# Storing the adaLN gates of a two-layer hybrid trunk: one transposed store a layer instead of column stores

## The chip, the core and the metric

The kernel runs on one core of a Trainium2 chip. The metric is device time in microseconds (us) of one execution; lower is better. The core has a matrix engine, TensorE (PE), and three engines for elementwise work, VectorE (DVE), ScalarE (ACT) and GpSimd (POOL). Each works through its own queue in order. Transfers are issued from SyncE (SP), from ACT and from POOL, and are moved by 16 DMA engines that all of these share. On-chip tiles have 128 partitions; what PE writes goes to PSUM, everything else is in SBUF or in device memory (DRAM).

## The reference

Two trunk layers run over 512 latent tokens and 256 context tokens, each of width 1024. Each layer begins by modulating its input with vectors that depend on the conditioning, and ends by gating its output with another of these vectors:

```
mod   = silu(c)     @ mod_w[l] + mod_b[l]        # 3 x 1024: shift, scale, gate (latents)
mod_c = silu(c_ctx) @ mod_w[l] + mod_b[l]        # the same for the context tokens
z   = (rmsnorm(x, pre_g) * (1 + scale) + shift) @ w_in
y_mla, y_pool, y_gla = attention(z), pooling mixer(z), gated linear attention(z)
out = (g_m * (y_mla @ w_bm) + g_p * (y_pool @ w_bp) + g_g * (y_gla @ w_bg)) @ w_out
x   = x + gate * rmsnorm(out, post_g)
```

The context stream does the same with mod_c, in layer 0 only; layer 1 uses the context for keys, values and states but does not produce it. The result is the latent stream after layer 1.

## The kernel before

All large products are made in three terms from operands that are split into a high and a low part (`mm3`): ACT makes the high part (`wh`, `act`), DVE the low part (`wl`, `tt`). Weights come in loads of 512 KB, issued on SP (`load_raw`, line 106), into a ring of three buffers with the tag "raw" in the pool `stream`; the split frees the buffer.

In each layer the projection is computed in blocks (`z_A`, `z_B`; the merge gates are the blocks `zA_m`, weights `raw_m`), staged through the pool `stage` (tag "st", two buffers) and written to DRAM by POOL's queue. The merge gates are interleaved with the attention heads (queries, scores `sc`, softmax `pe`, transposes `pt`, weighted sums `av`). Then the three branches are projected and merged (`br_p`, `br_g`, `br_m`; their inputs `yp`, `yg`, `ym` are reloaded through the same "raw" ring), and last come the output projection (`zB_wo`, `wo`), the post norm, the gate and the residual.

The function `modulation(l)` computes the 3072 modulation values of layer l in twelve chunks of 256 columns. Chunks 0 to 3 are the shift, 4 to 7 the scale, 8 to 11 the gate. It is a generator, and the layers advance it at fixed places. Layer 0's first eight chunks are made on PE at the start of the program. All others are made beside PE (`chunk_beside_pe`): the weight chunk comes in two halves through the "raw" ring (`raw_mod`), DVE and POOL accumulate 128 partial sums (`macc`), and four or eight small products with a column of ones (`modt`, in a PSUM tile of the pool `psz`, tag "z", two buffers) sum over the partitions. So the result stands as columns: partition p, column b holds value 128 b + p. The function `columns` adds the bias and, for the gate chunks, multiplies with the post norm's gain; the result lies in `cols` (in the profile `mcols`), for two streams (latents and context; in layer 1's gate chunks only the latents).

Shift and scale are used as columns. The gate is needed as a row that is the same on all partitions, since it multiplies tiles whose partitions are tokens. For that, each gate chunk is written to a DRAM tensor `grow` of shape 2 x 1024, one store per stream, each from 128 partitions with two values of 4 bytes (line 180):

```
nc.gpsimd.dma_start(out=grow[st].rearrange("(b p) -> p b", p=P)[:, 2 * j - 16:2 * j - 14], in_=dst[:, :, st])
```

and before the output projection `gate_rows` (line 265) reads each row back, the same 4 KB to all 128 partitions, into the tile `pg`. `pg` is used in the multiplications of `part` and `xo` by the gate (lines 1056 and 1072).

Layer 0's four gate chunks, the eight chunks of layer 1's shift and scale, and the first of its gate chunks are made in layer 0, beside its attention and at the start of its merge; the other three gate chunks of layer 1 are made in layer 1, beside the projection of the pooling branch.

The order of the instructions on every engine is not the order of the text: a planner reorders the whole program when it is built, from simulated times of the instructions and from priorities that the text sets (`urgent`).

Of the kernel before, what the change touches and what calls it, by code (L numbers as in the profile page):

```python
# [11 lines left out]
F32 = mybir.dt.float32  # L12
# [6 lines left out]
P = 128  # L19
D = 1024  # L20
KD = 8
# [4 lines left out]
DEPTH = 2  # L26
# [22 lines left out]
def hybrid_kernel(ctx, tc, io, out):  # L49
    nc = tc.nc  # L50
    V, S, G, PE = nc.vector, nc.scalar, nc.gpsimd, nc.tensor
# [8 lines left out]
    stage = ctx.enter_context(tc.tile_pool(name="stage", bufs=2))  # L60
    small = ctx.enter_context(tc.tile_pool(name="small", bufs=4))
    dram = ctx.enter_context(tc.tile_pool(name="dram", bufs=1, space=MemoryType.DRAM))
    psz = ctx.enter_context(tc.tile_pool(name="psz", bufs=2, space=MemoryType.PSUM))
# [3 lines left out]
    def act(out, in_, func=AF.Copy, **kw):  # L67
        return S.activation(out=out, in_=in_, func=func, **kw)  # L68

    def tt(out, a, b, op=ALU.mult, eng=None):  # L70
        return (eng or V).tensor_tensor(out=out, in0=a, in1=b, op=op)  # L71

    def stt(out, a, s, b, op0=ALU.mult, op1=ALU.mult):
        return V.scalar_tensor_tensor(out=out, in0=a, scalar=s, in1=b, op0=op0, op1=op1)  # L74
# [13 lines left out]
    def mm(out, lhsT, rhs, start, stop):  # L88
        PE.matmul(out=out, lhsT=lhsT, rhs=rhs, start=start, stop=stop)  # L89
# [14 lines left out]
    def load_raw(src, nk, width, name, pool=stream):  # L104
        raw = pool.tile([P, nk, width], F32, tag="raw", name=f"raw_{name}", bufs=3 if pool is stream else None)
        nc.sync.dma_start(out=raw, in_=src)
        return raw
# [17 lines left out]
    ident = const.tile([P, P], F32, name="ident")  # L125
# [29 lines left out]
    def modulation(l, pool=None):  # L155


        cols = const.tile([P, 24, 2], F32, tag=f"mcols{l}", name=f"mcols{l}")
        grow = dram.tile([2, D], F32, name=f"grow{l}")
        mods[l] = (cols, grow)  # L160
        modb = small.tile([P, 24], F32, tag="modb", name=f"modb{l}", bufs=1)
        nc.gpsimd.dma_start(out=modb, in_=io["mod_b"][l])
        pre = small.tile([P, KD], F32, tag="pre", name=f"pre{l}", bufs=1)
        nc.gpsimd.dma_start(out=pre, in_=io["pre_norm"][l])
        post = small.tile([P, KD], F32, tag="post", name=f"post{l}", bufs=1)
        nc.gpsimd.dma_start(out=post, in_=io["post_norm"][l])

        def columns(j, pt, streams=2):

            at = slice(2 * j, 2 * j + 2)  # L170
            dst = cols[:, at, 0:streams]

            def spread(v, c0):
                return v[:, 2 * j - c0:2 * j - c0 + 2].unsqueeze(2).to_broadcast([P, 2, streams])

            tt(dst, pt[:, :, 0:streams], spread(modb, 0), ALU.add)
            if j >= 8:
                tt(dst, dst, spread(post, 16))
                for st in range(streams):
                    nc.gpsimd.dma_start(out=grow[st].rearrange("(b p) -> p b", p=P)[:, 2 * j - 16:2 * j - 14], in_=dst[:, :, st])  # L180
            elif j >= 4:

                stt(dst, dst, 1.0, spread(pre, 8), ALU.add, ALU.mult)

        def chunk_on_pe(j):
            parts = j in (5, 6, 3, 7)
            ps = pst.tile([4 if parts else 2, 256], F32, tag="t", name=f"modps{l}_{j}")
            for half in range(2):
                raw = pool.tile([P, 4, 256], F32, tag="raw", name=f"raw_mod{l}_{j}_{half}", bufs=10)
                nc.sync.dma_start(out=raw, in_=io["mod_w"][l, j][:, 4 * half:4 * half + 4, :])  # L190
                if parts:
                    wh = pool.tile([P, 4, 256], F32R, tag="xin", name=f"mwh{l}_{j}_{half}", bufs=6)
                    wl = pool.tile([P, 4, 256], F32R, tag="xin", name=f"mwl{l}_{j}_{half}", bufs=6)
                    act(wh, raw)
                    tt(wl, raw, wh.bitcast(F32), ALU.subtract)
                for k in range(4):
                    kk = 4 * half + k
                    if parts:
                        mm(ps, chl[:, kk, :], wh[:, k, :], kk == 0, False)
                        mm(ps[0:2], chl[:, kk, 0:2], wl[:, k, :], False, kk == KD - 1)  # L200
                    else:
                        mm(ps, csil[:, kk, :], raw[:, k, :], kk == 0, kk == KD - 1)
            n = 4 if parts else 2
            row = pool.tile([n, 256], F32, tag="modrow", name=f"modrow{l}_{j}")
            act(row, ps)
            pt = psz.tile([P, 2, 2], F32, tag="z", name=f"modt{l}_{j}")
            for i in range(2):
                mm(pt[:, i], row[:, i * P:(i + 1) * P], sel[0:n], True, True)
            columns(j, pt)

        def chunk_beside_pe(j):

            streams = 2 if j < 8 or l < DEPTH - 1 else 1
            acc = small.tile([P, 2, 256], F32, tag="macc", name=f"macc{l}_{j}", bufs=1)
            for half in range(2):
                raw = load_raw(io["mod_w"][l, j][:, 4 * half:4 * half + 4, :], 4, 256, f"mod{l}_{j}_{half}")
                for k in range(4):
                    kk = 4 * half + k
                    for st in range(streams):
                        c = csil[:, kk, st:st + 1]  # L220
                        w, a = raw[:, k], acc[:, st]
                        eng = (G if streams == 1 and kk%2 else V) if st==0 else (G if kk%2 else V)
                        if kk == 0:
                            (eng if eng is G else V).tensor_scalar(out=a, in0=w, scalar1=c, scalar2=None, op0=ALU.mult)
                        elif eng is V:
                            stt(a, w, c, a, ALU.mult, ALU.add)
                        else:
                            if eng is S:
                                act(w, w, scale=c)
                            else:  # L230
                                G.tensor_scalar(out=w, in0=w, scalar1=c, scalar2=None, op0=ALU.mult)  # L231
                            tt(a, a, w, ALU.add, G)
            yield
            pt = psz.tile([P, 2, 2], F32, tag="z", name=f"modt{l}_{j}")
            for i in range(2):
                for st in range(streams):
                    mm(pt[:, i, st:st + 1], acc[:, st, i * P:(i + 1) * P], ones, True, True)
            columns(j, pt, streams)


        pend = []
        for j in (0, 4, 1, 5, 2, 6, 3, 7, 8, 9, 10, 11):
            if pool is not None and j < 8:
                chunk_on_pe(j)
            else:
                pend.append(chunk_beside_pe(j))
                next(pend[-1])
                if len(pend) > 1:
                    next(pend.pop(0), None)
            if j == 11 or (pool is None and j == 7):  # L250
                yield
                for chunk in pend:
                    next(chunk, None)
                pend = []
            yield

    mods = {}

    def gate_rows(l, pool, streams):

        grow = mods[l][1]
        res = []
        for s in range(streams):
            pgt = pool.tile([P, D], F32, tag=f"pg{s}", name=f"pg{l}_{s}", bufs=1)
            nc.gpsimd.dma_start(out=pgt, in_=grow[s].partition_broadcast(P))
            res.append(pgt)
        return res

# [81 lines left out]
    def layer(l, hT, close_hT, side, todo_mod):  # L350
# [680 lines left out]
        op = g6.enter_context(opened(f"outp{l}", 2, side))  # L1031
        psw = g6.enter_context(opened(f"psw{l}", 4, None, MemoryType.PSUM))
        pgr = gate_rows(l, op, 2 if full else 1)
        part = op.tile([P, NT, 512], F32, tag="part", name=f"part{l}", bufs=1)
        order = [2, 3, 4, 5] + ([0, 1] if full else [])
# [74 lines left out]
    sp = g0.enter_context(opened("start", 2, "left"))  # L1110
    psx = g0.enter_context(opened("psx", 4, None, MemoryType.PSUM))
    mod0 = modulation(0, sp)
    xin = {}
    for t in (2, 3, 4, 5, 0, 1):
# [28 lines left out]

    close_hT, side = gh.close, "left"
    todo_mod = chain(mod0, *(modulation(l) for l in range(1, DEPTH)))
    for l in range(DEPTH):
        hT, close_hT = layer(l, hT, close_hT, side, todo_mod)
# [108 lines left out]
```

## Time and profile before

| | |
|---|---|
| median of 3 runs | 1515.74 us (1512.39 to 1519.95) |
| the profiled execution | 1514.81 us, span 1513.0 us |
| granted TensorE clock, mean | 0.984 |
| busy: PE, PEld, DVE, ACT, POOL | 95%, 85%, 71%, 47%, 34% |
| moved by DMA | 209.75 MB, mean 139 GB/s |
| stores to grow (line 180) | 12, 1.0 KB each, issue to landing 9.4 us in the median |
| reads of grow (line 265) | 3, 512 KB each, 4.7 us in the median |

The profile is of one execution. PEld is PE's loading of the stationary operand, which overlaps with its products. An instruction's row names its line, its operation and the tiles it writes and reads (`out<-in`); where a helper issues it, the line is the helper's (line 68 is `act`, 71 `tt`, 74 `stt`, 89 `mm`). In square brackets stands how long the engine was idle before the instruction and which engine, line and tile ended that wait. In tables by window the busy time of each engine is followed by the number of its instructions, and after the engines come the granted clock of TensorE (1.00 is full speed), the busy share of the 16 DMA engines and the GB/s that they moved. For transfers the time from issue to landing is given.

### The profile page before, as it was taken

The page shows a single profiled execution, that of the slowest core. Times are in us where ns is not written, and L with a number is a line of the kernel's source. Part 1 is how long each engine was busy: PE and PEld are TensorE (multiplying, and loading weights), DVE is VectorE, ACT ScalarE, POOL GpSimd, SP SyncE. Part 2 cuts the span into 40 slices and gives each one's busy share as a digit, 9 for nine tenths or more (in the row PEclk, how much of TensorE's full clock was granted, in tenths as well). Part 3 has the DMA queues.
Part 4 walks back from the last instruction along what each step waited for, and adds up shares of the span by engine and source line. Part 5 has one row for each costly group of instructions (what it writes and reads, how often), then busy time and mean ns, then how long its engine had stood idle before and what let it go on. Part 6 is the DMA issues. An engine that isn't in the chain of part 4 may idle for free.

```text
span 1513.0 us, 23911 instructions
## 1 busy us (share of the span) xinstructions
PE 1444.7 (95%) x8940; PEld 1279.7 (85%) x8940; DVE 1066.7 (71%) x1980; ACT 717.3 (47%) x1340; POOL 521.8 (34%) x695
## 2 busy tenths in 40 slices
PE   7999999999997999997999999999999999998988
PEld 4799899998886889886879988988988888886778
DVE  3645999757576788876676373789976676686783
ACT  6554453343334445666443345654253555454532
POOL 3432333444243443542111064414463100053550
PEclk9999999999998999998999999999999999999999
DMA  9333323256544532346565234334356523157731
GB/s 366 108 125 113 107 96 115 90 166 192 183 74 101 144 118 90 130 147 163 173 210 198 82 126 129 124 127 127 100 180 204 164 96 96 51 151 145 232 132 69
DMA packets 64195, 209.75 MB, mean 139 GB/s; under 512 B 12464, under 2 KB 15696, under 8 KB 64080
## 3 DMA queue, kind: packets, MB, share of 16 engines
q1 hardware_dynamic: 38688, 116.74, 25.2%
q0 software_dynamic: 24528, 88.34, 18.3%
q10 hardware_dynamic: 864, 3.15, 0.5%
q8 instruction: 70, 1.15, 0.3%
q14 instruction: 45, 0.37, 0.1%
HBM read 161.65 MB, written 46.54 MB: 138 GB/s over the span
## 4 chain that ended last, share of the span: by engine, by line
PE 63%; issue 11%; DVE 11%; DMA 8%; POOL 3%; ACT 3%; POOLq 0%; DVEq 0%; SPq 0%; ACTq 0%
PE zA_m L89 13%; PE zB_gv L89 5%; PE zA_px L89 4%; PE zA_mg L89 4%; PE zB_wo L89 4%; PE wo L89 3%; DMA raw_m<-in_w_in 3%; PE lv L89 3%; PE zA_pg L89 3%; PE zA_gk L89 2%; PE br_p L89 2%; PE br_m L89 2%; PE br_g L89 2%; PE zB_qkv L89 2%; PE zA_gq L89 2%
## 5 line engine op out<-in xcount | busy, mean ns | idle before, releaser
L89 PE MATMUL zA_m<-hh,wh_m 128*128 128x512 f32 (+1 forms) x576 | 206.6, 359 | 1.0 <-ACT wh_m L68 1.0
L89 PE MATMUL zA_m<-hh,wl_m 128*128 128x512 f32 (+1 forms) x576 | 206.7, 359 | 0.6 <-DVE wl_m L71 0.6
L89 PE MATMUL zA_m<-hl,wh_m 128*128 128x512 f32 (+1 forms) x576 | 206.5, 359 | 0.0
L89 PEld LDWEIGHTS zA_m<-hh,wh_m 128*128 128x128 f32 x576 | 110.1, 191 | 16.0 <-ACT wh_m L68 1.4
L89 PEld LDWEIGHTS zA_m<-hh,wl_m 128*128 128x128 f32 x576 | 109.9, 191 | 15.6 <-DVE wl_m L71 1.1
L89 PEld LDWEIGHTS zA_m<-hl,wh_m 128*128 128x128 f32 x576 | 109.9, 191 | 14.4
L68 ACT ACTIVATE wh_m<-raw_m 128x1024 fp32r<-128x1024 f32 x48 | 50.9, 1060 | 93.0 <-PE zA_m L89 45.5
L68 ACT ACTIVATE pe<-sc,mx 128x768 f32<-128x768 f32 (+1 forms) x80 | 65.2, 814 | 60.2 <-DVE mx L831 59.7
L831 DVE TENSOR_REDUCE mx<-sc 128x1 f32<-128x768 f32 (+1 forms) x80 | 67.7, 846 | 34.7 <-PE sc L89 34.0
L71 DVE TENSOR_TENSOR wl_m<-raw_m,wh_m 128x1024 fp32r<-128x1024 f32 x48 | 59.0, 1228 | 45.6 <-ACT wh_m L68 45.1
L231 POOL TENSOR_SCALAR raw_mod<-raw_mod,csil 128x256 f32<-128x256 f32 x64 | 69.2, 1085 | 62.0 <-DVE macc L74 38.5
L74 DVE SCALAR_TENSOR_TENSOR macc<-raw_mod,csil,macc 128x256 f32<-128x256 f32 x132 | 70.8, 547 | 12.4 <-POOL macc L71 10.5
L68 ACT ACTIVATE pth<-pt 128x256 fp32r<-128x256 f32 (+1 forms) x144 | 61.8, 471 | 34.6 <-PE pt L853 34.0
L71 DVE TENSOR_TENSOR ptl<-pt,pth 128x256 fp32r<-128x256 f32 (+1 forms) x144 | 72.6, 534 | 7.2 <-ACT pth L68 6.2
L89 PEld LDWEIGHTS lv<-pqk 128*128 128x128 f32 x560 | 70.8, 191 | 4.7 <-issue 1.8
L347 POOL DMA_DIRECT2D sm<-st_m x32 | 17.6, 550 | 165.5 <-ACT st_m L68 148.1
L89 PE MATMUL lv<-pqk 128*128 128x128 f32 x560 | 73.4, 275 | 1.3 <-DVE pqk L71 1.2
L89 PE MATMUL sc<-kth,qth 96*128 96x256 f32 (+1 forms) x144 | 50.8, 353 | 19.0 <-ACT pe L68 18.9
L71 POOL TENSOR_TENSOR macc<-macc,raw_mod 128x256 f32<-128x256 f32 x64 | 55.1, 860 | 36.4 <-DVE macc L74 30.6
L89 PE MATMUL br_p<-yp,wh_wbp 128*128 128x512 f32 (+1 forms) x192 | 56.3, 376 | 8.6 <-ACT yp L68 6.8
L853 PE MATMUL pt<-ident,pe 128*128 128x128 f32 x416 | 61.3, 273 | 0.7 <-ACT pe L68 0.7
L89 PE MATMUL zB_gv<-wh_gv,hh 128*128 128x256 f32 x192 | 55.7, 291 | 4.1 <-ACT st_gv L68 2.1
(402 smaller groups left out, 4732.8 us busy)
## 6 DMA issues: line engine op xcount, KB each, us to landing
raw_mod<-in_mod_w SPq DMA_DIRECT2D x48, 512.0 KB, 5.0
raw_m<-in_w_in SPq DMA_DIRECT2D x48, 512.0 KB, 3.8
sm<-st_m POOLq DMA_DIRECT2D x24, 384.0 KB, 2.9
raw_wo<-in_w_out SPq DMA_DIRECT2D x16, 512.0 KB, 4.0
sm<-st_m POOLq DMA_DIRECT2D x24, 256.0 KB, 2.5
raw_gv<-in_w_gv SPq DMA_DIRECT2D x8, 512.0 KB, 4.6
raw_gg<-in_w_in SPq DMA_DIRECT2D x8, 512.0 KB, 4.0
raw_px<-in_w_in SPq DMA_DIRECT2D x8, 512.0 KB, 3.7
```

The lines of the kernel that those rows point to most:

```text
L68: return S.activation(out=out, in_=in_, func=func, **kw)
L71: return (eng or V).tensor_tensor(out=out, in0=a, in1=b, op=op)
L74: return V.scalar_tensor_tensor(out=out, in0=a, scalar=s, in1=b, op0=op0, op1=op1)
L89: PE.matmul(out=out, lhsT=lhsT, rhs=rhs, start=start, stop=stop)
L231: G.tensor_scalar(out=w, in0=w, scalar1=c, scalar2=None, op0=ALU.mult)
L347: nc.gpsimd.dma_start(out=dst[:, lo:T], in_=st[:, lo:T])
L831: V.tensor_reduce(out=mx, in_=ps[:, 0:nkey], axis=AX.X, op=ALU.max, negate=True)
L853: PE.transpose(out=pt[:, kk, :], in_=pe[:, (k0 + kk) * P:(k0 + kk + 1) * P], identity=ident)
```

## The change

The twelve column stores go. `grow` gets the shape 8 x streams x 128, with two streams in layer 0 and one in layer 1. After the last gate chunk of a layer, PE transposes the gate columns (128 x 16 in layer 0, 128 x 8 in layer 1) into a PSUM tile of `psz`, ACT copies the 16 or 8 rows of 128 values into a tile of `stage`, and one store on POOL's queue writes them to `grow`. The reads in `gate_rows` follow the new layout: a row of 1024 values lies in DRAM as eight pieces of 128 values, in layer 0 every second such piece, in layer 1 one behind the other.

```diff
@@ modulation
-        grow = dram.tile([2, D], F32, name=f"grow{l}")
+        grow = dram.tile([KD, 2 if l < DEPTH - 1 else 1, P], F32, name=f"grow{l}")
@@ columns
             if j >= 8:
                 tt(dst, dst, spread(post, 16))
-                for st in range(streams):
-                    nc.gpsimd.dma_start(out=grow[st].rearrange("(b p) -> p b", p=P)[:, 2 * j - 16:2 * j - 14], in_=dst[:, :, st])
@@ modulation, the loop over chunks
                 for chunk in pend:
                     next(chunk, None)
                 pend = []
+            if j == 11:
+
+                n = KD * grow.shape[1]
+                pt = psz.tile([n, P], F32, tag="z", name=f"gateT{l}")
+                columns_ = cols[:, 16:24, :].rearrange("p b s -> p (b s)") if n > KD else cols[:, 16:24, 0]
+                PE.transpose(out=pt, in_=columns_, identity=ident)
+                row = stage.tile([P, P], F32, tag="st", name=f"gates{l}")
+                act(row[0:n], pt)
+                nc.gpsimd.dma_start(out=grow.rearrange("b s p -> (b s) p"), in_=row[0:n])
             yield
@@ gate_rows
-            nc.gpsimd.dma_start(out=pgt, in_=grow[s].partition_broadcast(P))
+            nc.gpsimd.dma_start(out=pgt.rearrange("q (b p) -> q b p", p=P), in_=grow[:, s].partition_broadcast(P))
```

## The prediction

> **What bounds the kernel now.** I read the page's busy times first, then the idle stretches of TensorE in the tables by window, then for each long stretch the releaser in the timelines, and last the transfers under way at that moment.
>
> ```profile
> PE 1444.7 (95%) x8940; PEld 1279.7 (85%) x8940; DVE 1066.7 (71%) x1980; ACT 717.3 (47%) x1340; POOL 521.8 (34%) x695
> ```
>
> TensorE (PE) is busy 95% of the span, so it sets the time, and a saving has to come from its idle time or its clock. The three longest holes that have a gate store just ahead of them look like this (columns: window, its length, busy time of PE, PEld, DVE, ACT, POOL, then granted clock, busy share of the DMA engines, GB/s):
>
> ```profile
> 444.00:452.60 8.60, 8.60 (x53) 7.56 (x51) 7.92 (x13) 1.55 (x5) 3.72 (x5) 1.00 1.00 35
> 452.60:462.90 10.30, 0.08 (x2) 0.04 (x1) 1.07 (x1) 2.13 (x4) 0.00 (x0) 0.67 0.52 85
> 462.90:466.50 3.60, 3.60 (x16) 3.60 (x17) 3.15 (x8) 1.15 (x3) 1.47 (x1) 0.51 0.42 146
> ...
> 699.40:706.30 6.90, 0.07 (x2) 0.02 (x1) 1.00 (x2) 0.70 (x2) 1.74 (x3) 0.69 0.65 122
> 706.30:712.20 5.90, 5.89 (x17) 4.68 (x18) 4.59 (x11) 5.33 (x12) 0.28 (x1) 0.50 0.76 253
> ...
> 1373.30:1378.10 4.80, 0.05 (x2) 0.03 (x1) 0.93 (x1) 2.01 (x4) 0.00 (x0) 0.97 0.59 206
> 1378.10:1384.70 6.60, 6.20 (x18) 5.14 (x19) 6.38 (x11) 4.96 (x9) 3.75 (x4) 0.51 0.57 167
> ```
>
> PE stands still for 10.2, 6.8 and 4.8 us, and each time it restarts at half clock. Ahead of the first hole the 16 DMA engines are busy all the time (share 1.00) and yet move 35 GB/s. What ended each hole, and what POOL had issued before:
>
> ```profile
> 443.70 1.48 POOL L180 DMA_DIRECT2D grow<-mcols  x2
> 460.74 1.06 ACT L68 ACTIVATE wh_m<-raw_m 128x1024 fp32r<-128x1024 f32 x1 [13.88 <-DMA raw_m<-in_w_in]
> 461.82 0.90 ACT L68 ACTIVATE pe<-sc,mx 128x768 f32<-128x768 f32 x1
> 462.87 0.58 PE L89 MATMUL sc<-kth,qth 96*128 96x256 f32 x1 [10.22 <-ACT pe L68]
> ...
> 692.75 0.74 POOL L180 DMA_DIRECT2D grow<-mcols  x1 [0.32 <-DVE mcols L71]
> 705.60 1.88 ACT L68 ACTIVATE yp<-yrp 128x512 fp32r<-128x512 f32 x4 [7.40 <-DMA yrp<-yp]
> 706.28 1.81 PE L89 MATMUL br_p<-yp,wh_wbp 128*128 128x512 f32 x3 [6.83 <-ACT yp L68]
> ...
> 1363.63 0.75 POOL L180 DMA_DIRECT2D grow<-mcols  x1
> 1376.09 1.06 ACT L68 ACTIVATE wh_wbp<-raw_wbp 128x1024 fp32r<-128x1024 f32 x1 [10.04 <-DMA raw_wbp<-in_w_branch_p]
> 1378.08 0.80 PE L89 MATMUL sc<-kth,qth 96*128 96x512 f32 x1 [4.75 <-ACT pe L68]
> ```
>
> The pattern is the same three times: POOL issues a store to grow, ScalarE (ACT) then waits 7 to 14 us for a load that should be quick, and PE waits behind ACT, because ACT works its queue in order (the softmax pe of the first and third hole sits behind the split of the weights). Issue to landing, first over the whole run, then in the windows around the three stores (440 to 462, 690 to 699, 1360 to 1370):
>
> ```profile
> L180 POOL DMA_DIRECT2D grow<-mcols x12: 716/742/776, 426.4 to 1387.1; - x12
> DMA to landing us min/median/max: 7.1/9.4/16.6
> ...
> raw_m<-in_w_in SPq DMA_DIRECT2D x48, 512.0 KB, 3.8
> raw_wbp<-in_w_branch_p SPq DMA_DIRECT2D x8, 512.0 KB, 4.5
> sm<-st_m POOLq DMA_DIRECT2D x24, 384.0 KB, 2.9
> DMA to landing us min/median/max: 2.5/3.0/10.9
> ...
> raw_m<-in_w_in SPq DMA_DIRECT2D x1, 512.0 KB, 16.2
> sm<-st_m POOLq DMA_DIRECT2D x1, 384.0 KB, 12.6
> raw_wbp<-in_w_branch_p SPq DMA_DIRECT2D x1, 512.0 KB, 11.2
> ```
>
> The first two rows are those of the stores at L180: 1 KB each, 9.4 us in the median. The second "DMA to landing" row is that of yrp. While such a store is under way, loads that take 3 to 4.5 us take 11 to 16. So the stores of 256 packets of 4 bytes hold the DMA engines, everything queued beside them waits, and PE runs dry where it has too little in hand. That it can have enough is seen beside two others, with PE busy throughout:
>
> ```profile
> 483.39 1.51 POOL L180 DMA_DIRECT2D grow<-mcols  x2
> 483.00:493.00 10.00, 10.00 (x60) 8.68 (x59) 9.62 (x22) 5.67 (x14) 8.21 (x10) 1.00 0.51 60
> ...
> 1346.90 0.76 POOL L180 DMA_DIRECT2D grow<-mcols  x1 [0.31 <-DVE mcols L71]
> 1346.90:1356.40 9.50, 9.50 (x57) 8.29 (x56) 9.36 (x19) 3.68 (x9) 6.47 (x8) 1.00 0.49 69
> ```
>
> So the price of a store is what PE lacks at that moment, not its 9 us; I count only the three holes.
>
> **The change part by part.**
>
> *Removed: twelve stores (eight in layer 0, four in layer 1).* POOL is relieved of 12 x 0.74 us = 8.9 us of issuing (the median in the row of L180). POOL is 34% busy and ends none of the three holes, so I count that at nothing; it only brings the macc sums behind the stores forward by 0.7 to 1.5 us.
>
> The holes, one by one, with what is late next:
>
> ```profile
> 444.53 0.33 SPq L106 DMA_DIRECT2D raw_m<-in_w_in  x1
> ...
> 689.96 16.98 SPq L935 DMA_DIRECT2D yrp<-yp  x4
> ...
> 1356.28 8.87 SPq L106 DMA_DIRECT2D raw_wbp<-in_w_branch_p  x2
> ```
>
> Hole 1. raw_m, issued at 444.53, lands after 3.8 us at 448.3; the split (1.06) and the softmax behind it (0.90, both rows above) are done by 450.3, before PE needs them at 452.65. DVE's half of the split is next; DVE is busy 7.92 of the 8.6 us up to 452.6, so it comes perhaps 0.5 us late. Recovered: 10.22 of waiting, and 3.6 us at clock 0.51 that cost 3.6 x 0.49 = 1.8: 12.0 - 0.5 = 11.5 us.
>
> Hole 2. The second of four yrp loads is the late one; at 3.0 us it lands at about 698.2 and PE asks for it at 699.45. But the loads share a ring of three buffers (tag "raw") with the last weights of the modulation, so they come one at a time, load 3.0 plus ACT's split of 0.94 (half of the 1.88 above) apiece, and the four cannot all be there at 700. I leave 3.5 us of the hole standing: 6.83 + 5.9 x 0.50 - 3.5 = 6.3 us.
>
> Hole 3. The second raw_wbp is issued at 1356.28 + 8.87 - 0.33 = 1364.8 and lands after 4.5 at 1369.3; split and softmax take 2 us, to 1371.3, before PE needs them at 1373.3. Recovered: 4.75 + 6.6 x 0.49 = 8.0 us.
>
> Together 11.5 + 6.3 + 8.0 = 25.8 us. Of it the half clock is 1.8 + 2.95 + 3.2 = 7.95. The Trainium skill, page "TensorE: Matmul & The Clock Gate", Part 1, says that about 3.4 us of work after an idle window run at half clock; that is an estimate of 1.7 us a restart, 5.1 in all, and a sum 2.9 us smaller. Of the three restarts here one agrees (3.6 us), two last 5.9 and 6.6, so I stay with the rows.
>
> *Added: one transpose, one copy and one store of rows per layer.* PE's work is small:
>
> ```profile
> L853 PE MATMUL pt<-ident,pe 128*128 128x128 f32 x416 | 61.3, 273 | 0.7 <-ACT pe L68 0.7
> 1380.16 0.85 PE L89 MATMUL modt<-ones,macc 128*128 128x1 f32 x4
> ...
> 1386.60 0.16 DVE L71 TENSOR_TENSOR mcols<-mcols,post 128x2 f32<-128x2 f32 x1
> ```
>
> 2 x 0.27 = 0.5 us of PE. The wait matters more: the transpose needs the last product with post, and PE works in order, so whatever stands behind the transpose waits for DVE too. In layer 1 that product ended 1386.76 - 1381.01 = 5.75 us after modt. The wait lies between 0 (the planner puts it late enough) and 5.75 a layer; the planner reckons with DVE's queue as well, so I take the lower part, 1 us a layer. The transpose takes one of the two "z" buffers of PSUM that the zA blocks turn over, and the copy one of the two "st" buffers, behind which a later evacuation (st_m) may wait for a landing of 2.9: between 0 and 2.9 a layer, and I put it inside that 1 us, since stage_out does the same dozens of times beside a busy PE. The new stores are 16 and 8 rows of 512 bytes; their POOL issue is bounded by 0.74. Total 0.5 + 2 = 2.5 us.
>
> *Moved: the gates are stored once, after the last chunk.* The reader is far behind:
>
> ```profile
> 816.87 0.53 POOL L265 DMA_DIRECT2D pg<-grow  x1 [1.46 <-PE br_g L89]
> L71 DVE TENSOR_TENSOR part<-part,pg x10: 684/692/693, 845.0 to 1485.9; 128x512 f32<-128x512 f32 x10
> osg<-sgg POOLq DMA_DIRECT2D x10, 256.0 KB, 3.5
> ```
>
> Layer 0 has stored long before 692.75, where layer 1's first store stands, and reads at 816.87. In layer 0 the read now takes 1024 pieces of 512 bytes where it took 128 of 4 KB. The nearest row is osg, 512 pieces of 512 bytes in 3.5 us; twice that is at most 7 us, and the first use is at 845.0, 28 us after the issue. I cost it at nothing; without that cover it would be 2 x 7 = 14 us. Layer 1's rows lie side by side, so its read is as before.
>
> *Sum.* 25.8 - 2.5 = 23.3. The profiled execution took 1514.81 us (span 1513.0), 0.9 under the median 1515.74. 1514.8 - 23.3 = 1491.5; I put 1492. The bounds: all three holes with their clock (21.8 + 7.95 = 29.7) and no cost give 1485; the short holes beside them could add a few us, so 1482. Holes closed by half and both waits at the transposes at their upper end give 1514.8 - 14.9 + 12 = 1512; I take 1508 as the upper end for 8 in 10.
>
> One term has no row. The order on every engine comes from a planner that reckons the whole program with times of its own; with twelve stores fewer it may come out another way from about 425 us on. I give it no sign; its size is bounded by one hole like these, 8 to 12 us either way.
>
> **The rivals.**
>
> *Partial.* The loads become quick, but another wait takes over: the ring of three raw buffers, which POOL's slow sums release, or PE standing at the transposes. For it: hole 2, where four loads share the ring. Against it: in holes 1 and 3 the late load had already been issued 8 us or more before PE ran dry. It recovers 8 to 17 us: 1498 to 1507, say 1503.
>
> *No change.* The loads are late for a reason that stays (the ring, the planner's order), and the stores only fall in the same stretch. Then the cost of 2.5 remains: 1517. For it: beside the stores at 483 and 1347 PE has no hole. Against it: loads with a landing of 11 to 16 us stand beside stores each time, with the DMA engines full at 35 GB/s. The Trainium skill, page "DMA: Bandwidth & Descriptors", section "Anatomy of one DMA", gives about 2.0 us plus bytes over 436 GB/s for a transfer issued from GpSimd, so a store of 1 KB would take 2.0 us and hold up little; by that rule this rival would be the forecast. The trace has 9.4 us, and I go by it.
>
> *Slower.* The pieces of 512 bytes do to the loads what those of 4 bytes did. A store's 256 pieces are 16 for each of 16 engines in 9.4 - 2.9 = 6.5 us, 0.41 us a piece; 64 pieces each would be 26 us, twice 52, beginning at 817 beside the loads of w_out. The readers of pg are covered until 845, 28 us, the weights that are loaded beside it by little, so the stall is between 24 and 52; with the middle, 38, and 3 of clock, 1492 + 41 = 1533. It is slower by half a per cent from about 0.33 us a piece on. Against it: osg moves 512 such pieces in 3.5 us, some 0.1 us a piece at most.
>
> **How the numbers follow.** Forecast, 1483 to 1498: 0.60. Partial, 1498 to 1508: 0.22. No change: 0.11. Slower: 0.05. More than the three holes, under 1483: 0.02. Half a per cent, which is about what a measurement of this kernel can tell, is 7.6 us: faster means below 1508, slower above 1523. So faster 0.84, same 0.11, slower 0.05. The range 1482 to 1508 leaves out the last cases.
>
> **What would show it.** Right: no load of 512 KB in layer 0's attention above some 7 us; the holes near 452 and 1373 gone, with no half clock there; a shorter one near 700; the landing of grow near 3 us; pg under 8 us; two new transposes with less than 2 us of PE idle ahead of them. Wrong: holes of the same size with normal landings (then the order is to blame), landings still long with no grow store beside them, or PE idle for several us at the transposes with DVE's mcols as the releaser.

## The result, and the profile after

| | before | after |
|---|---|---|
| median | 1515.74 us (1512.39 to 1519.95) | 1492.08 us (1491.12 to 1495.41) |
| profiled execution, span | 1514.81, 1513.0 us | 1491.12, 1489.3 us |
| granted clock, mean | 0.984 | 0.987 |

The ratio is 0.985, with a 95% interval of 0.9829 to 0.9871: the change saves 23.7 us. The total came out as predicted (1492). The experiments below show that this rests partly on two errors that cancel.

The busy times on the page of the kernel after (engine, busy us, share of the span, instructions):

```profile
PE 1439.0 (97%) x8942; PEld 1276.7 (86%) x8942; DVE 1064.9 (72%) x1980; ACT 717.9 (48%) x1342; POOL 518.1 (35%) x685
```

PE has two matmuls more (the transposes) and is still 5.7 us less busy, which fits the half clock that is gone: work at half clock counts as longer. The other 18 us of the span were idle time of PE. The windows around the places of the three old holes, in the kernel after (columns as before: window, length, PE, PEld, DVE, ACT, POOL, granted clock, DMA share, GB/s):

```profile
440.00:460.00 20.00, 20.00 (x123) 17.75 (x123) 18.27 (x37) 9.37 (x22) 11.46 (x10) 1.00 0.37 126
460.00:480.00 20.00, 17.45 (x103) 15.22 (x102) 11.93 (x27) 7.62 (x17) 5.60 (x6) 0.91 0.31 99
...
680.00:700.00 20.00, 17.17 (x96) 14.76 (x95) 15.49 (x34) 14.74 (x33) 4.96 (x7) 0.83 0.66 199
700.00:720.00 20.00, 18.96 (x122) 17.00 (x121) 14.40 (x26) 13.65 (x25) 1.63 (x3) 1.00 0.58 184
...
1360.00:1380.00 20.00, 18.16 (x102) 15.61 (x103) 17.06 (x25) 12.91 (x23) 10.07 (x14) 1.00 0.76 247
1380.00:1400.00 20.00, 19.63 (x105) 16.43 (x104) 14.18 (x23) 11.72 (x21) 11.29 (x11) 1.00 0.65 208
```

No window has more than 3 us of idle PE, and none the mark of the jam, DMA engines full at 35 GB/s. Half clock is left, though, as the mean clocks of 0.91 and 0.83 say: the trace's record of the clock has 0.5 for 3.41 us from 473.11 on, for 3.41 us from 497.00 and for 6.83 us from 684.73, each beside short waits of PE. The longest wait of PE left there, and the two at the new transposes, from the timeline of PE in the kernel after:

```profile
471.94 0.50 PE L89 MATMUL sc<-kth,qth 96*128 96x512 f32 x1 [2.38 <-ACT pe L68]
497.21 0.38 PE L258 MATMUL gateT<-ident,mcols 128*16 128x128 f32 x1 [0.25 <-DVE mcols L71]
1364.02 0.28 PE L258 MATMUL gateT<-ident,mcols 128*8 128x128 f32 x1 [1.67 <-DVE mcols L71]
```

Issue to landing in the kernel after, one row for each tile, in the order raw_m, yrp, raw_wbp, the two stores of rows to grow, and the three reads into pg:

```profile
DMA to landing us min/median/max: 3.1/3.7/6.1
...
DMA to landing us min/median/max: 2.6/3.3/4.4
...
DMA to landing us min/median/max: 3.2/3.8/5.8
...
DMA to landing us min/median/max: 2.7/4.1/5.6
...
DMA to landing us min/median/max: 4.7/6.4/7.4
L272 POOL DMA_DIRECT2D pg<-grow x3: 564/884/914, 804.1 to 1425.5; - x3
```

The slowest raw_m, yrp and raw_wbp land in 6.1, 4.4 and 5.8 us; beside the column stores the late ones of before took 11 to 16. The last row is POOL's time to issue a read of pg: 0.88 to 0.91 us for the two with 1024 pieces, where it was 0.53 before.

### The profile page after: what moved, and what is told of

Read it like the earlier page. It is cut to its first block, busy times and chain, and to the rows that moved or that the text cites. A ratio compares the mean times of both kernels' runs of the same rounds, so it can differ in the third digit from the quotient of the medians.

```text
span 1489.3 us, 23924 instructions
## 1 busy us (share of the span) xinstructions
PE 1439.0 (97%) x8942; PEld 1276.7 (86%) x8942; DVE 1064.9 (72%) x1980; ACT 717.9 (48%) x1342; POOL 518.1 (35%) x685
## 2 busy tenths in 40 slices
DMA packets 63875, 209.74 MB, mean 141 GB/s; under 512 B 12120, under 2 KB 15376, under 8 KB 63760
## 3 DMA queue, kind: packets, MB, share of 16 engines
q1 hardware_dynamic: 38688, 116.74, 23.7%
## 4 chain that ended last, share of the span: by engine, by line
PE 64%; issue 13%; DVE 9%; DMA 6%; POOL 5%; ACT 3%; POOLq 0%; SPq 0%; DVEq 0%; ACTq 0%
PE zA_m L89 12%; PE zB_gv L89 5%; PE zB_wo L89 4%; PE zA_px L89 4%; PE zA_mg L89 4%; PE wo L89 3%; PE br_m L89 3%; PE lv L89 3%; PE zA_pg L89 3%; PE br_g L89 2%; PE zA_gk L89 2%; PE zB_qkv L89 2%; PE zA_gq L89 2%; PE br_p L89 2%; PE modps L89 2%
## 5 line engine op out<-in xcount | busy, mean ns | idle before, releaser
L229 POOL TENSOR_SCALAR raw_mod<-raw_mod,csil 128x256 f32<-128x256 f32 x64 | 73.5, 1152 | 51.5 <-DVE macc L74 27.1
L74 DVE SCALAR_TENSOR_TENSOR macc<-raw_mod,csil,macc 128x256 f32<-128x256 f32 x132 | 66.8, 522 | 7.0 <-POOL macc L71 5.6
L89 PE MATMUL av<-pth,vv 128*128 128x256 f32 x208 | 56.1, 294 | 0.7 <-ACT pth L68 0.7
L860 PEld LDWEIGHTS pt<-ident,pe 128*128 128x128 f32 x416 | 49.7, 143 | 8.3 <-ACT pe L68 1.6
```

Source lines behind the costliest of these rows:

```text
L860: PE.transpose(out=pt[:, kk, :], in_=pe[:, (k0 + kk) * P:(k0 + kk + 1) * P], identity=ident)
```

## Experiments

Three questions were open. Was it the stores that made the loads late, or the planner's order, which changed with them? If the stores, was it that their pieces are small and many, or that they lie next to each other in DRAM? And is the sum made of the terms that the prediction named? Times are medians; each ratio, with its 95% interval, is to the kernel before timed beside it on the same chip (1514.40 us for e1 to e4, 1514.47 for e5 to e8, 1516.03 for e9 to e11). e7, e8 and e9 have two runs each, and those of e7 lie 7.5 us apart (1483.73 and 1491.27).

| run | median, us | ratio |
|---|---|---|
| e1_back | 1519.45 | 1.0027 (1.0011 to 1.0044) |
| e2_scatter | 1485.12 | 0.9802 (0.9774 to 0.9829) |
| e3_sbuf | 1484.46 | 0.9799 (0.9775 to 0.9822) |
| e7_step64 | 1487.50 | 0.9819 (0.9784 to 0.9853) |
| e8_step16 | 1485.39 | 0.9805 (0.9785 to 0.9824) |
| e9_step8 | 1492.44 | 0.9844 (0.9806 to 0.9883) |
| e10_old_order | 1481.48 | 0.9771 (0.9746 to 0.9796) |
| e4_layer0 | 1520.92 | 1.0049 (1.0030 to 1.0068) |
| e5_layer1 | 1493.70 | 0.9869 (0.9848 to 0.9890) |
| e6_late | 1499.76 | 0.9895 (0.9878 to 0.9912) |
| e11_urgent | 1493.60 | 0.9853 (0.9825 to 0.9880) |

### The stores, and where they go

e1 is the kernel after with the twelve column stores put back, into a DRAM tensor that nothing reads. e2 writes the same 4-byte pieces 512 bytes apart, e3 writes them into SBUF. All three have the same order on every engine; only the addresses of the stores differ.

```diff
+        spare = dram.tile([2, D], F32, name=f"spare{l}")             # e1
+        spare = dram.tile([2, P, KD, 128], F32, name=f"spare{l}")    # e2
 ...
                 tt(dst, dst, spread(post, 16))
+                for st in range(streams):
+                    nc.gpsimd.dma_start(out=OUT, in_=dst[:, :, st])
 # e1: OUT = spare[st].rearrange("(b p) -> p b", p=P)[:, 2*j-16:2*j-14]
 # e2: OUT = spare[st][:, 2*j-16:2*j-14, 0]
 # e3: OUT = csig[:, 2*j-16:2*j-14, st]
```

> The changed kernel, and beside the new store of rows the twelve column stores again, into a DRAM tensor that nothing reads. Theory J (the stores of 4-byte pieces hold the DMA engines, and PE runs dry behind loads that are late): their issue to landing is 9 us or more again, several loads beside them take over 9 us, at least two holes of PE of over 4 us come back, and the time is 1505 to 1520. Theory O (the planner's new order closed the holes, or POOL's shorter queue): the order has changed again, so the time can be anything, but it must then equal that of the next kernels that have the same order, whatever their destination.

> As the kernel with the column stores back, and every instruction in the same order on every engine, but the pieces of 4 bytes go to places 512 bytes apart in DRAM, so that no two pieces fall into one line. Theory J1 (each 4-byte write to DRAM costs an engine its time, wherever it goes): landing 8 us or more, time within 4 us of the kernel with the stores back. Theory J2 (it is writes of several engines into the same line that wait for one another): landing under 5 us and time 1490 to 1497.

> As the kernel with the column stores back, the same order on every engine, the same twelve stores of 256 pieces of 4 bytes, but into an SBUF tile that nothing reads any more, not into DRAM. Theory J: landing under 5 us, no hole of PE over 3 us that has such a store ahead of it, time 1490 to 1498. Theory O: within 3 us of the kernel with the stores back, since order, issues and waits are the same. A third outcome, landing over 8 us here too, would say that the number of pieces alone is the cost and DRAM has no part in it.

e1 lost all of the gain and 5 us more than that; e2 and e3 were 34.3 and 35.0 us faster than e1. They also ended 5 us below the ranges given for them (1490 to 1497 and 1490 to 1498), for which the planner's order, treated further below, is the reason. The transfers issued between 444 and 462 us, beside the first layer-0 stores (tile, queue, count, size, median us to landing), in e1, then e2, then e3:

```profile
raw_m<-in_w_in SPq DMA_DIRECT2D x1, 512.0 KB, 11.5
spare<-mcols POOLq DMA_DIRECT2D x2, 1.0 KB, 9.8
...
raw_m<-in_w_in SPq DMA_DIRECT2D x2, 512.0 KB, 3.4
spare<-mcols POOLq DMA_DIRECT2D x2, 1.0 KB, 2.7
...
raw_m<-in_w_in SPq DMA_DIRECT2D x2, 512.0 KB, 3.3
csig<-mcols POOLq DMA_DIRECT2D x2, 1.0 KB, 2.4
```

With the same instructions in the same order, the weight load takes 11.5 us beside adjacent pieces and 3.4 beside pieces that lie apart. PE sees it, in e1's timeline:

```profile
461.72 0.58 PE L89 MATMUL sc<-kth,qth 96*128 96x256 f32 x1 [5.65 <-ACT pe L68]
```

The hole of the yrp loads is back too, with 6.82 us at 705.90. So the jam is real and is made by the stores, not by the order. It is not made by 256 pieces of 4 bytes as such: e2 has as many, as small, to the same memory, and they cost nothing that shows. They must be neighbours.

Nor are they 256 packets, as the prediction has it. The page of e1 counts 384 packets more than that of the kernel after (64259 and 63875), 32 for each store. In the packet records a store is 16 packets of 64 bytes and 16 of 4; those of 64 bytes take some 40 ns each, in e1 as in e2. The long packets are those of the loads: one of 4 KB takes up to 5.1 us between 446 and 457 us in e1, and at most 0.64 us between 446 and 454 us in e2. So the trace shows the time on the traffic beside the stores, and does not show what holds it.

### How near is near

e7, e8 and e9 are e2 with pieces 64, 16 and 8 bytes apart.

```diff
-        spare = dram.tile([2, P, KD, 128], F32, name=f"spare{l}")
+        spare = dram.tile([2, KD, P, 16], F32, name=f"spare{l}")    # e7; 4 in e8, 2 in e9
 ...
-  out=spare[st][:, 2*j-16:2*j-14, 0]
+  out=spare[st].rearrange("b p m -> p b m")[:, 2*j-16:2*j-14, 0]
```

> As the kernel with the column stores back, the same order on every engine, with the pieces of 4 bytes 64 bytes apart in DRAM (adjacent ones jam, ones 512 bytes apart do not). If what they fight over is 64 bytes or less: landing 2.5 to 3.5 us, 1483 to 1488. If it is a unit of 512 bytes with the pieces in it one after the other (6.7 us for 128 in one, 0.05 a piece): 8 in each, landing still under 4 and the time much the same. Landing over 6 us would mean a unit far larger.

> The same with the pieces 16 bytes apart, a quarter as many in any unit as when adjacent. If pieces in one unit wait for one another: landing 2.8 + 6.7 / 4 = 4.5 us, 3.5 to 6, and the time 1484 to 1495. If only adjacent pieces (sharing 16 bytes or less) conflict: landing under 3.3 us. If it is all or nothing within a line of 64 bytes: landing 9 us and some 1519.

> As the kernel with the column stores back, the same order on every engine, with the pieces of 4 bytes 8 bytes apart in DRAM, between the adjacent ones (landing 9.5 us) and those 16 bytes apart (3.4 us). If pieces that share a unit wait for one another: 2.8 + 6.7 / 2 = 6.1 us, 4.5 to 7.5, and the time 1487 to 1508. If the conflict is among neighbours within 8 bytes alone: under 4 us and 1483 to 1489.

Landing of the twelve stores with pieces 4 (e1), 8 (e9), 16 (e8), 64 (e7) and 512 bytes apart (e2), one row each:

```profile
DMA to landing us min/median/max: 7.2/9.5/10.8
...
DMA to landing us min/median/max: 3.5/6.2/8.0
...
DMA to landing us min/median/max: 2.0/3.4/6.4
...
DMA to landing us min/median/max: 2.0/2.6/4.5
...
DMA to landing us min/median/max: 2.2/2.8/4.3
```

Above 2.6 us, 6.9, 3.6 and 0.8 us are left at 4, 8 and 16 bytes: half at the first doubling, less than a quarter of that at the second. The 6.2 us at 8 bytes came as expected (6.1), the 3.4 at 16 bytes fell below the 4.5 that was expected. The times follow in the main: 8 bytes costs about 8 us against e3 (1491.47 and 1493.40, though one run of e7 came as high), 16 bytes nothing that shows. The landing grows the closer the pieces lie, so pieces that share a short stretch of DRAM seem to wait for one another; the length of that stretch, and why the writes wait for each other, no run here settles. In the Trainium skill, page "DMA: Bandwidth & Descriptors", the section "Specifications" sets 512 bytes as the least transfer for line rate and names a read-modify-write below it. Size alone does not decide here: pieces of 4 bytes land in 2.6 us once they are 64 bytes apart. On the same page of the Trainium skill, the 2.0 us plus bytes over 436 GB/s of "Anatomy of one DMA" come near that, and miss the adjacent ones by 7.5 us.

### The old order without the jam

e10 is the kernel before, in its exact order on all engines, with its stores 512 bytes apart. The read of pg takes rows of the input x instead of grow, so the gates are left out of its result.

```diff
-        grow = dram.tile([2, D], F32, name=f"grow{l}")
+        grow = dram.tile([2, KD, P, P], F32, name=f"grow{l}")
 ...
-  out=grow[st].rearrange("(b p) -> p b", p=P)[:, 2*j-16:2*j-14]
+  out=grow[st].rearrange("b p m -> p b m")[:, 2*j-16:2*j-14, 0]
 ...
-            nc.gpsimd.dma_start(out=pgt, in_=grow[s].partition_broadcast(P))
+            nc.gpsimd.dma_start(out=pgt, in_=io["x"][s].partition_broadcast(P))
```

> The kernel before with every instruction in its old order, the twelve column stores of 4-byte pieces among them, but the pieces lie 512 bytes apart in DRAM; pg is read from rows of the input x, 4 KB to each partition as before, so the gates are left out and the output is not gated rightly. It takes the jam out of the old order and changes nothing else. Theory J with the prediction's terms: the three holes go but for 4 us, 1514.5 - 25.8 = 1489, between 1481 and 1495; landing of the stores under 4 us. Theory O (the old order itself makes the holes): 1508 or more, with holes of 4 us and more near 452, 700 and 1373.

It took 1481.48 us, 34.5 less than the kernel before: that is the price of the jam in that order. Since the order is the same, each matmul has its twin, and the difference of their starts says where the time is saved. The twins of those that restarted after the three holes, and the last matmul, in e10's timeline of PE, and last of all the twin of that last matmul in the kernel before:

```profile
453.69 0.28 PE L89 MATMUL sc<-kth,qth 96*128 96x256 f32 x1
...
685.38 0.60 PE L89 MATMUL br_p<-yp,wh_wbp 128*128 128x512 f32 x2
...
1348.27 0.47 PE L89 MATMUL sc<-kth,qth 96*128 96x512 f32 x1
...
1469.99 0.28 PE L89 MATMUL wo<-wh_wo,ml 128*128 128x256 f32 x1
...
1505.62 0.28 PE L89 MATMUL wo<-wh_wo,ml 128*128 128x256 f32 x1
```

| | e10's lead ahead of the hole, us | at the restart | after the half clock | worth |
|---|---|---|---|---|
| hole 1 | -1.20 (452.37 and 453.57) | 9.18 | 10.84 | 12.0 |
| hole 2 | 13.83 (699.18 and 685.35) | 20.90 | 21.72 | 7.9 |
| hole 3 | 24.81 (1373.05 and 1348.24) | 29.81 | 33.15 | 8.3 |
| all else | | | 35.63 at the last matmul | 7.4 |

The three holes are worth 28.2 of the 35.6 us. The rest came in small amounts, 3.0 between holes 1 and 2, 3.1 between holes 2 and 3, 2.5 after hole 3, less the 1.2 ahead of hole 1. The table sets one execution of each kernel against one of the other. Between 800 and 1000 us, around the read of pg, whose source differs too, the lead grows by 1.5 us (20.9 to 22.4); none of the three holes lies there.

### Where the kernel after stands against it

The kernel after is 10.6 us slower than e10 in the medians, and 11.9 in the profiled executions (spans 1489.3 and 1477.4 us). Its transposes account for 2.6: 0.66 us of matmul and 0.25 + 1.67 us of waiting, in the rows above. Most of the rest shows in the window from 420 to 690 us, here in the kernel before, the kernel after, e10 and e3:

```profile
420.00:690.00 270.00, 256.70 (x1629) 230.18 (x1628) 211.64 (x439) 136.81 (x296) 118.11 (x134) 0.97 0.42 116
...
420.00:690.00 270.00, 261.44 (x1655) 233.99 (x1655) 214.29 (x448) 139.94 (x306) 116.93 (x132) 0.98 0.36 120
...
420.00:690.00 270.00, 264.87 (x1700) 237.25 (x1699) 223.51 (x465) 148.20 (x323) 124.81 (x141) 0.99 0.38 127
...
420.00:690.00 270.00, 264.74 (x1701) 237.46 (x1700) 219.41 (x461) 146.92 (x319) 126.97 (x142) 0.99 0.38 125
```

e3 contains everything that the kernel after does, and twelve harmless stores more, and is 7.6 us faster in the median (5.7 in the profiled executions, spans 1483.6 and 1489.3). In this window it gets 46 matmuls more done, about 7 us at its mean of 0.16 us each, although neither has a jam. The two differ in nothing but those stores and the order that the planner makes. PE's order in the kernel after departs from that of before at 433 us, just behind the first store that is gone (426.4); e3, which still has stores at these places, keeps it 360 matmuls longer, until its first transpose comes due. So dropping the stores made the planner choose an order that is about 8 us worse.

How it costs that much can be read off. In the window PE has 3.3 us less busy time in the kernel after (261.44 and 264.74). The rest is mostly clock: by 690 us it has had 12.1 us at half clock in the three stretches named above, of which an estimated 6 are lost; e3 has one, 3.41 us from 538.54 on, worth 1.7. None of the waits beside the three stretches is longer than 2.38 us. e11 below, which has the same order, has half clock at the same three places (from 472.09, 499.40 and 687.13). Which exchange of places makes these waits stays open; no run changed the order by itself.

### One layer alone

e4 makes the change in layer 0 alone, e5 in layer 1 alone; the other layer keeps its column stores.

```diff
+        turned = l == 0        # e5: l == 1
 ...
+                if not turned:
+                    (the two lines of the column stores)
 ...
-            if j == 11:
+            if j == 11 and turned:
```

> The change in layer 0 alone; layer 1 keeps its four column stores. Theory J with the prediction's terms: hole 1 is worth 11.5 and the transpose costs 1.25, so 1515.7 - 10.3 = 1505.5, between 1501 and 1509, with the holes near 700 and 1373 (some 12 us earlier) still there. Theory O: no sum of parts; a time outside 1498 to 1511 would speak for it.

> The change in layer 1 alone; layer 0 keeps its eight column stores. Terms of the prediction: holes 2 and 3 (14.3 us) go, the transpose costs 1.25, so 1515 - 13 = 1502, between 1498 and 1507, with a hole near 452 still there. If the parts added up to the whole (-23.7, with layer 0 alone at +6), it would be 1485. Theory N (a store costs what PE lacks just then, so the parts need not add up): a hole of 6 us or more in layer 0's attention beside one of the eight stores, none over 3 us near 700 and in layer 1, time 1495 to 1508.

Both missed: e4 was 6.5 us slower than before where 1505 was expected, e5 20.8 us faster where 1502 was expected. The first row is e4's place of hole 2 in PE's timeline, then the landing of yrp in e4; the last two rows are e5's place of hole 1 and the landing of raw_m in e5:

```profile
703.16 1.01 PE L89 MATMUL br_p<-yp,wh_wbp 128*128 128x512 f32 x2 [9.84 <-ACT yp L68]
...
DMA to landing us min/median/max: 2.6/3.2/11.5
...
459.57 0.58 PE L89 MATMUL sc<-kth,qth 96*128 96x256 f32 x1 [5.44 <-ACT pe L68]
...
DMA to landing us min/median/max: 3.1/3.8/11.3
```

e4 has the order of the kernel after until 691 us, and then its first layer-1 store makes a hole of 9.84 us, longer than the 6.83 of before; three more, of 4.17, 3.79 and 4.69 us, follow in layer 1. With the four stores, e4 is 29 us slower than the kernel after; from 691 us on its order is its own, so that not all of this need be the stores'. In e5 the eight stores of layer 0 stand where they stood, since its order is that of before until 1381 us, but hole 1 is 5.44 us instead of 10.22. A hole is thus no fixed price of a store: it is how far the landing of one load runs beyond what PE has in hand, and that moves with a few us of position. Why the same place gave 10.2 us in one execution and 5.4 in the other, one profile each cannot say.

### The waits at the transposes

e6 moves transpose, copy and store into `gate_rows`, just ahead of the read. e11 marks transpose and copy as urgent for the planner.

```diff
 # e6
-            if j == 11:
-                (transpose, copy, store)
 ...
-        grow = mods[l][1]
+        cols, grow = mods[l]
+        (transpose, copy, store)
 # e11
-                PE.transpose(out=pt, in_=columns_, identity=ident)
+                with urgent():
+                    PE.transpose(out=pt, in_=columns_, identity=ident)
 ...
-                act(row[0:n], pt)
+                with urgent():
+                    act(row[0:n], pt)
```

> The changed kernel with the transpose, the copy and the store of rows moved to just ahead of the reads, before the output projection, where the gate columns have long been ready. If the waits at the transposes are what the change costs: 1 to 3 us under the changed kernel, 1489 to 1491, and no PE idle ahead of gateT. If the order that the planner makes matters more (7 us lie between two kernels with harmless stores): anywhere from 1483 to 1497. The round trip of the rows through DRAM, now some 3 + 6 us ahead of the first use of pg, should cost nothing.

> The changed kernel with the transpose and the copy put ahead by the priority that the other evacuations have. It gives the planner's order another throw, with the jam gone. If the order is worth some 7 us either way: 1483 to 1500. If the changed kernel's 1492 is set by the waits at the transposes: under 1490 with less than 1 us of PE idle ahead of gateT, or over 1494 with more than 3 us there.

The transposes in PE's timeline, layer 1's of e6 first, then both of e11:

```profile
1439.59 0.38 PE L263 MATMUL gateT<-ident,mcols 128*8 128x128 f32 x1 [4.72 <-DVE gated L74]
...
499.27 0.30 PE L259 MATMUL gateT<-ident,mcols 128*16 128x128 f32 x1 [0.25 <-DVE mcols L71]
1369.78 0.28 PE L259 MATMUL gateT<-ident,mcols 128*8 128x128 f32 x1 [0.62 <-DVE mcols L71]
```

e6 was to gain 1 to 3 us and lost 7.7, which is also above the wider range given for it (1483 to 1497). The columns have long been there, but now PE stands 4.72 us ahead of the transpose until DVE's merge (`gated`) is done; in the kernel after its wait there is 1.70 us, ahead of zB_wo. No row gives the rest.

e11 tests nothing of what it was made for. The traces show the same instructions in the same order on every engine as in the kernel after, so marking transpose and copy as urgent changed nothing, and e11 is the kernel after once more: 1493.60 against 1492.08 us. It shows how far two executions of one order lie apart. The wait at the transpose of layer 1 is 1.67 us in one and 0.62 in the other, while the one with the shorter wait is the longer by 4.8 us (1495.95 and 1491.12). The waits at the transposes are thus small beside the spread; that they cost nothing is not shown.

## Why the prediction was right, and where its sum was not

*The bound and the mechanism.* Right. The stores make the loads late, the loads hold ACT, and ACT holds PE: e1 against e3 shows it with everything else equal. "256 packets of 4 bytes" was the wrong description of the cause, though. Neither count nor size jams, as e2 shows, but that the pieces adjoin in DRAM. "The DMA engines full at 35 GB/s", given for all three stores, holds ahead of hole 1 alone; ahead of holes 2 and 3 the share is 0.65 at 104 GB/s and 0.96 at 52:

```profile
690.00:699.40 9.40, 8.19 (x53) 6.67 (x51) 6.78 (x17) 5.65 (x13) 2.78 (x4) 1.00 0.65 104
...
1364.00:1373.30 9.30, 9.30 (x52) 7.70 (x50) 5.77 (x11) 1.67 (x5) 2.41 (x4) 1.00 0.96 52
```

*The holes.* Predicted 11.5 + 6.3 + 8.0 = 25.8, measured in e10 12.0 + 7.9 + 8.3 = 28.2. In hole 2, 3.5 us were left standing for the ring of three raw buffers, since the yrp loads were to come one at a time; of the 9.8 us that this hole and its clock were reckoned at, only 1.9 stayed. In e10 the second and the third load are issued 0.4 us apart (681.37 and 681.80), and the fourth has landed at 688.05. The clock's part, 7.95 in the prediction, measured 1.7 + 0.8 + 3.3 = 5.8 (the lead after the half clock less that at the restart). That is nearer to the 5.1 that was estimated from the Trainium skill, page "TensorE: Matmul & The Clock Gate", Part 1, but not because its 1.7 us a restart held: for holes 1 and 3 the rows gave 1.8 and 3.2, near the 1.7 and 3.3 measured. Only hole 2 came lower than the row, and there PE waits in e10 as well (busy 4.06 of the 5.20 us of the twin stretch, 685.30 to 690.50, at clock 1.00). The trace's record of the clock has half clock in blocks of 3.41 us, and more than one block around each hole: 10.24, 10.24 and 6.83 us. The waits more than made up for the clock: 22.4 us of them came back, where 17.9 were reckoned. e5 shows that this sum is no constant of the kernel: hole 1, 10.22 us in the profile before, was 5.44 there at the same place of the same order.

*The short holes.* This term was mis-sized. The prediction said that the price is what PE lacks and counted only three places, "a few us" beside them at most. e10 shows 8.6 us in the stretches between and after the holes.

*The planner's order.* It was given no sign and bounded at 8 to 12 us. It cost about 8, near the lower of those figures, and cancelled what the holes and the short holes brought beyond the sum. That the forecast hit the median is luck, owed to these together: without the reordering the change would have come to about 1484.5, where e3 stands, inside the range but 7.5 us under the forecast.

*The added work.* Predicted 2.5, measured 2.6: 0.66 us of PE and 1.92 of waiting, within the "1 us a layer"; in e11, the same order, 0.58 and 0.87. No row shows a cost of the "st" and "z" buffers.

*The read of pg.* Predicted at most 7 us and hidden; it landed in 7.4 at most, a little over, with its first use at 831.3, 27 us after the issue at 804.1. That POOL takes 0.88 to 0.91 us to issue it instead of 0.53 was not foreseen; what reads pg begins long after it.

*The rivals.* Partial did not happen: no new wait as long as the holes took their place, although the short ones of the new order brought half clock with them. No change fell with e1 and e3. Slower was argued from 0.41 us a piece, taken from the column stores. That price belongs to neighbouring writes, so the scaling to 512-byte reads had no ground, although the answer (unlikely) was right.

*What would show it.* No 512 KB load of raw_m above 6.1 us, no jammed window, two transposes with less than 2 us of idle PE: as said. The landing of grow came at 2.7 and 5.6 us for "near 3", and near 700 a wait of 1.04 us was left, with half clock ahead of it from 684.73 to 691.56.

## What to carry to other kernels

A small store that writes neighbouring elements one by one (a column written as a row) is priced by what waits behind it, not by its bytes; look for late loads beside it, and for DMA engines that are busy while they move little. Writing rows, or spreading the elements 16 bytes apart or more, takes the price away; what it would cost to read spread elements back was not measured here. Where a planner orders the program, an edit that removes instructions also buys a new order: compare with a kernel that keeps the old one before crediting the edit, make sure that a run meant to change the order did, and do not expect the parts of a change to add up.

## What the runs showed of the hardware that was not expected

Writes of 4 bytes cost by their neighbourhood: 9.5 us to land at 4 bytes apart, 6.2 at 8, 3.4 at 16, 2.6 at 64, 2.8 at 512 and 2.6 into SBUF, for the same 256 pieces. What they delay is other traffic, from a load of 3.4 us to one of 11.5, and over the whole kernel 34.5 us in the old order and 35.0 in e1's. The stores' own packets do not get longer by it, those of the loads do.

Half clock came in blocks of 3.41 us in all these traces, one to three of them (3.41, 6.83 or 10.24 us; the last stretch runs into the program's end). It does not need a long hole: in the kernel after, 6.83 us of it begin at 684.73, amid two waits of 0.69 and 1.37 us.

A faster version than the kernel after follows from the runs: e2 and e3 end at 1485.12 and 1484.46 us, with all of its work and twelve stores that nothing reads. What they gain is the planner's order, not a saving of work, so it holds for this program and not as a method.
